# Token rows gathered as whole float32, a two-group place second, side products in single runs, and clock-keeping products ahead of the counts

## The chip, the cores and the metric

The kernel runs on one core of one Trainium2 chip. The core has TensorE (PE: matmuls, PEld: the loads of their stationary operand), VectorE (DVE), ScalarE (ACT), GpSimd (POOL) and SyncE (SP), which here issues the transfers of weights. The metric is the time of one execution on the device in microseconds (us), the median of three runs.

## The reference

Two consecutive decoder layers over x of 256 tokens × 1024 channels in float32. The first has a convolution module and a linear recurrence side by side and a dense SwiGLU; the second a short convolution and block-sparse attention side by side, and then the part that the change concerns, top-2-of-8 SwiGLU experts:

```python
def moe_swiglu(h, router_w, router_b, wg, wu, wd):
    logits = xf.astype(F32) @ router_w.astype(F32) + router_b.astype(F32)
    top_logit, top_e = lax.top_k(logits, TOP_K)
    top_w = jax.nn.softmax(top_logit, axis=-1)
    ...
    def expert_block(args):
        xb, e = args
        return (jax.nn.silu(xb @ wg[e]) * (xb @ wu[e])) @ wd[e]
    ...
    out = jnp.zeros((n_tok, d), F32).at[row_tok].add(ys.astype(F32) * row_w[:, None])
```

`wg` and `wu` of an expert are 1024 × 3584, `wd` is 3584 × 1024, all float32: 42 MiB an expert, 336 MiB for the eight. Each is read once in each execution.

## The kernel before

The weights come as a stream of units (class `Stream`). An expert has 46 units: 16 of 1 MiB for the first 512-wide pieces of gate and up (phase 0 is gate, phase 1 up, 8 units each), 16 of 768 KiB for the 384-wide pieces (phases 2 and 3), and 14 of 1 MiB for `wd`. They land in slots of a ring; there are RING = 10 slots, and MORE = 6 more (`grow`) from the second half on. `fill` issues on SP's queue, in order, the transfer of unit n + ring as soon as PE has finished unit n (`finish`); the transfer is line 338.

The experts are ranked by their token counts, and a *place* is a position in the order in which they are computed. A place has room for two or three groups of 32 rows (`NGS`): an expert with few tokens goes to a place of two groups. `RANKS` says which rank by count goes to which place. The expert of the first place is guessed from the router's bias well before the counts (`S.first`), so its transfers can start early; the others are known once the counts are made, and SP reads their positions from `offs` (`values_load`, line 1279) and waits for it there.

In a place, each unit of gate and up runs with matmuls of four column groups, 128 × 32 stationary (`up`, line 1424), 24 records a unit with three groups, 16 with two. A float32 matmul leaves two records in the trace, one of type float32r (kept to its first part) leaves one. `down_e` (lines 1438 and 1445) does the same for `wd`.

Around these units stand *side products*, attached to the units by `after(e, phase, unit, f)`, which runs `f` behind that unit's matmuls of place e:

- `gather_bank` (line 1340): the rows of x of the next place or pair of places are gathered by a product with a matrix of ones and zeros, `G` (line 1315). The rows are held as two float32r parts, `hrh` and `hrl`, so each of the four banks has four products with the one and four with the other. `first_gather` does it for the first place.
- `backs` (lines 1377 and 1379): the transposes of `G` and the token weights, with which results go back.
- `scatter` (line 1404): the result of a place is added to x while the next place runs.

Ahead of the first place stands the routing: the last router products (line 1175), the selection `sel` on DVE (lines 1241 to 1243), the counts and the position of each token in its expert's rows by small products with `sel` (lines 1247 to 1252), `pos` (line 1254), `G`, and the gather. `keep_warm(20, …)` (line 550) issues 20 products whose result nobody reads, behind these small products. The scheduler puts instructions into an engine's row by readiness and priority; parts of it are pinned to the written order.

## Time and profile before

| | us |
|---|---|
| median of three runs (1347.02 to 1351.15) | 1349.56 |
| time of the profiled execution | 1347.33 |
| its span | 1345.6 |
| PE busy | 1274.1 (95%) |
| DVE busy | 492.8 (37%) |
| ACT busy | 301.6 (22%) |

The transfers moved 472.20 MB at a mean of 349 GB/s over the span. A busy PE is not a PE at its peak. Of the chain that ended last, PE has 80% and transfers 12%. The places of the experts begin on PE at 489.93, 605.66, 717.30, 801.89, 913.72, 1031.71, 1122.97 and 1240.23 us, and the last place's products end at 1335.2. Rows of a timeline group neighbouring instructions of one kind, with xN records; their busy times overlap a little, since matmuls are pipelined.

### The profile page before, as it was taken

How to read it: one execution, taken by the hardware profiler on the slowest of the kernel's cores; microseconds unless marked ns; L12 is line 12 of the kernel's file. 1: busy time of each engine (PE TensorE's matmuls, PEld its weight loads, DVE VectorE, ACT ScalarE, POOL GpSimd, SP SyncE). 2: the span in 40 equal slices, each digit the busy share in tenths (PEclk: the TensorE clock that was granted, in tenths of full speed). 3: DMA queues.
4: the chain of work that ended last, by engine and by line, in shares of the span. 5: the costliest groups of instructions: out<-in, count | busy, mean ns of one | idle time of the engine just before them, and what ended most of it. 6: DMA issues, size and time to landing. Idle time of an engine off the chain costs nothing.

```text
span 1345.6 us, 29781 instructions
## 1 busy us (share of the span) xinstructions
PE 1274.1 (95%) x12884; PEld 759.1 (56%) x12884; DVE 492.8 (37%) x1064; ACT 301.6 (22%) x623; POOL 1.2 (0%) x23
## 2 busy tenths in 40 slices
PE   4999999999999999999999999999999979999976
PEld 3878899999988863463354423353445312345321
DVE  8699998888777330101102001102101101100100
ACT  3175555555755322000001100000100000100000
POOL 0000000000000000000000000000000000000000
PEclk6998899999999979999999999999999999999999
DMA  9955999888400957999999999999999999999996
GB/s 380 401 200 210 360 372 357 306 339 342 180 7 33 373 220 256 384 417 405 358 417 417 417 419 417 416 418 417 416 418 416 416 419 419 414 417 417 401 414 232
DMA packets 72282, 472.20 MB, mean 351 GB/s; under 512 B 8272, under 2 KB 10320, under 8 KB 27856
## 3 DMA queue, kind: packets, MB, share of 16 engines
q1 hardware_dynamic: 72144, 470.22, 86.8%
q8 instruction: 103, 1.69, 0.5%
q14 instruction: 35, 0.29, 0.1%
HBM read 469.14 MB, written 1.05 MB: 349 GB/s over the span
## 4 chain that ended last, share of the span: by engine, by line
PE 80%; DMA 12%; DVE 6%; ACT 2%; issue 0%; DVEq 0%; SPq 0%; ACTq 0%
PE acc L1424 17%; PE mm L1424 17%; DMA raw<-in_moe 12%; PE mm L1445 8%; PE acc L1445 5%; PE mm L483 4%; PE mm L485 4%; PE mm L484 4%; PE acc L484 3%; PE acc L485 3%; PE acc L483 3%; PE mm L504 2%; PE acc L521 2%; DVE raw L468 1%; PE mm L1340 1%; DVE cv L795 1%
## 5 line engine op out<-in xcount | busy, mean ns | idle before, releaser
L1424 PE MATMUL acc<-raw,xe 128*32 128x512 f32 (+1 forms) x2688 | 264.8, 541 | 3.4 <-DMA raw<-in_moe 3.4
L1424 PE MATMUL mm<-raw,xe 128*32 128x512 f32 (+1 forms) x2688 | 260.8, 540 | 6.3 <-DMA raw<-in_moe 6.3
L1424 PEld LDWEIGHTS mm<-raw,xe 128*32 128x32 f32 x2688 | 84.9, 110 | 168.8 <-issue 145.7
L1424 PEld LDWEIGHTS acc<-raw,xe 128*32 128x32 f32 x2688 | 82.9, 110 | 150.2 <-issue 133.5
L367 ACT CAST wh<-raw 128x512 fp32r<-128x512 f32 x200 | 121.7, 620 | 128.3 <-PE mm L484 76.4
L368 DVE TENSOR_TENSOR wl<-raw,wh 128x512 fp32r<-128x512 f32 x200 | 133.8, 689 | 43.6 <-ACT wh L367 35.5
L483 PE MATMUL mm<-hh,wh 128*128 128x256 f32 x496 | 140.5, 284 | 0.5 <-ACT xr L657 0.5
L484 PE MATMUL mm<-hlo,wh 128*128 128x256 f32 x496 | 140.1, 283 | 0.3 <-DVE hlo L620 0.3
L485 PE MATMUL mm<-hh,wl 128*128 128x256 f32 x496 | 140.0, 283 | 0.0
L468 DVE SCALAR_TENSOR_TENSOR raw<-raw,crow 128x1024 f32<-128x1024 f32 x96 | 114.4, 1221 | 0.0
L1445 PE MATMUL mm<-raw,wh 128*32 128x256 f32 x2016 | 109.3, 379 | 0.0
L483 PEld LDWEIGHTS mm<-hh,wh 128*128 128x128 f32 x496 | 94.5, 191 | 1.4 <-ACT xr L657 0.7
L485 PEld LDWEIGHTS mm<-hh,wl 128*128 128x128 f32 x496 | 94.4, 190 | 1.1 <-issue 1.1
L484 PEld LDWEIGHTS mm<-hlo,wh 128*128 128x128 f32 x496 | 94.4, 191 | 1.1 <-issue 0.6
L1556 DVE TENSOR_TENSOR wl<-wl,acc 128x512 f32<-128x512 f32 (+1 forms) x22 | 13.1, 597 | 219.4 <-PE acc L1424 219.4
L1445 PEld LDWEIGHTS mm<-raw,wh 128*32 128x32 f32 x2016 | 65.4, 110 | 44.0 <-issue 1.2
L1556 DVE TENSOR_TENSOR wl<-wl,mm 128x512 f32<-128x512 f32 (+1 forms) x20 | 12.0, 598 | 181.3 <-PE mm L1424 181.3
L1445 PE MATMUL acc<-raw,wh 128*32 128x256 f32 x1344 | 72.9, 379 | 0.0
L1438 PE MATMUL acc<-raw,wh 128*32 128x512 f32 x448 | 54.3, 598 | 16.3 <-DMA raw<-in_moe 15.2
L504 PE MATMUL mm<-hh,raw 128*128 128x256 f32 x256 | 59.1, 393 | 4.0 <-ACT hh L612 4.0
L1445 PEld LDWEIGHTS acc<-raw,wh 128*32 128x32 f32 x1344 | 43.7, 110 | 29.3 <-issue 0.8
L504 PEld LDWEIGHTS mm<-hh,raw 128*128 128x128 f32 x256 | 50.4, 198 | 12.1 <-ACT hh L612 4.9
(346 smaller groups left out, 1225.2 us busy)
## 6 DMA issues: line engine op xcount, KB each, us to landing
raw<-in_moe SPq DMA_DIRECT2D x236, 1024.0 KB, 19.8
raw<-in_wst SPq DMA_DIRECT2D x109, 1024.0 KB, 7.0
raw<-in_moe SPq DMA_DIRECT2D x128, 768.0 KB, 15.0
raw<-in_moe SPq DMA_DIRECT2D x8, 512.0 KB, 14.7
x<-in_xt SPq DMA_DIRECT2D x1, 1024.0 KB, 5.0
out<-x SPq DMA_DIRECT2D x8, 128.0 KB, 2.7
gw<-in_gates SPq DMA_DIRECT2D x1, 512.0 KB, 19.5
mask<-in_const SPq DMA_DIRECT2D x1, 192.0 KB, 5.1
```

The costliest lines, as they stand in the source:

```text
L367: self.nc.scalar.copy(h, t[:, j:j + PART])
L368: self.nc.vector.tensor_tensor(l, t[:, j:j + PART], h.bitcast(F32), op=OP.subtract)
L468: nc.vector.scalar_tensor_tensor(src, src, 1.0, crow, op0=OP.mult, op1=OP.mult, accum_out=raw_mod[pre][:, 2 * n + b:2 * n + b + 1])
L483: nc.tensor.matmul(o, wh, xh, start=first, stop=False, skip_group_check=skip)
L484: nc.tensor.matmul(o, wh, xl, start=False, stop=False, skip_group_check=skip)
L485: nc.tensor.matmul(o, wl, xh, start=False, stop=last, skip_group_check=skip)
L504: nc.tensor.matmul(o, wh, xh[:, k], start=(cb == 0 and k == 0), stop=(k == KB - 1), skip_group_check=True)
L521: nc.tensor.matmul(o, wh, yf[:, k], start=st, stop=sp, skip_group_check=True)
L1424: nc.tensor.matmul(ps[j * GROUP:(j + 1) * GROUP, :width], xe[:, k, r * GROUP:(r + 1) * GROUP], w[:, j * width:(j + 1) * width], start=(k = ...
L1438: nc.tensor.matmul(yb[0][t * GROUP:(t + 1) * GROUP], hs[r], w[:, f * D + h * 512:f * D + (h + 1) * 512], start=first, stop=last, skip_grou ...
L1445: nc.tensor.matmul(yb[c // 2][t * GROUP:(t + 1) * GROUP, c % 2 * 256:c % 2 * 256 + 256], hs[r], w[:, f * D + q * 256:f * D + q * 256 + 256 ...
L1556: nc.vector.tensor_tensor(h, h, ps[:, :width], op=OP.mult)
```

## The change

The rows to be gathered are held once, as float32 (`hr`), so a bank has four float32 products instead of eight of float32r, and the six DVE operations that made `hrl` are gone. `keep_warm` stands ahead of the first products with `sel`, the count product behind `pos`. The places have two groups at 1, 4 and 7 (counted from 0) instead of 2, 5 and 7. Four gather banks stand behind one unit, so do the two `backs`, and the four scatter banks. The ring has MORE = 7, 17 slots in all.

```diff
...
-RING, AHEAD, PARTS, MORE, SPARE = 10, 3, 7, 6, 2
+RING, AHEAD, PARTS, MORE, SPARE = 10, 3, 7, 7, 2
...
-NGS = (3, 3, 2, 3, 3, 2, 3, 2)
-RANKS = (0, 1, 5, 2, 3, 6, 4, 7)
+NGS = (3, 2, 3, 3, 2, 3, 3, 2)
+RANKS = (0, 5, 1, 2, 6, 3, 4, 7)
...
-                        sq = ob.tile([P, 3, P], F32, name="sq", bufs=2)
+                        sq = ob.tile([P, 3, P], F32, name="sq")
...
-    hrh = mo.tile([P, 2, D], F32R, name="hrh")
-    hrl = mo.tile([P, 2, D], F32R, name="hrl")
+    hr = mo.tile([P, 2, D], F32, name="hr")
...
-        rests = []
         for g in range(3):
             for t in range(2):
                 r, n = row(t, g)
-                hh, hlo = (a[:, t, g * 384:g * 384 + n * P].rearrange("p (b c) -> p b c", b=n)
-                           for a in (hrh, hrl))
-                nc.scalar.activation(hh, r[:, :, :P], AF.Copy, scale=rr[:, t:t + 1])
-                rests.append((hlo, r[:, :, :P], rr[:, t:t + 1], hh.bitcast(F32)))
+                o = hr[:, t, g * 384:g * 384 + n * P].rearrange("p (b c) -> p b c", b=n)
+                nc.scalar.activation(o, r[:, :, :P], AF.Copy, scale=rr[:, t:t + 1])
...
-        chosen = nc.vector.tensor_scalar(sel, sel, 1.5, None, op0=OP.is_lt)
-
+        nc.vector.tensor_scalar(sel, sel, 1.5, None, op0=OP.is_lt)
+
+        keep_warm(WARM[1], ident, x[:, KB - 1, :P])
         pp = acc_bank()
-        for t in range(2):
-            nc.tensor.matmul(pp[:, 2 * NE:3 * NE], one_pp, sel[:, t], start=(t == 0), stop=(t == 1))
-
         below = con("below")
         nc.tensor.matmul(pp[:, :NE], below, sel[:, 0], start=True, stop=True)
         nc.tensor.matmul(pp[:, NE:2 * NE], below, sel[:, 1], start=True, stop=False)
@@ -1254,10 +1248,12 @@
         nc.vector.scalar_tensor_tensor(pos, pp[:, :2 * NE].rearrange("p (t e) -> p t e", t=2), 1.0,
                                        sel, op0=OP.add, op1=OP.mult)
 
+        for t in range(2):
+            nc.tensor.matmul(pp[:, 2 * NE:3 * NE], one_pp, sel[:, t], start=(t == 0), stop=(t == 1))
+
         t0 = mo.tile([P, 2, NE], F32, name="hid0")
         nc.vector.tensor_tensor(t0, pos, lead_[:, None].to_broadcast([P, 2, NE]), op=OP.mult)
         nc.vector.tensor_reduce(posp[:, :, 0], t0, axis=AX.X, op=OP.add)
-        keep_warm(WARM[1], ident, x[:, KB - 1, :P])
         nc.vector.tensor_copy(cnt, pp[:, 2 * NE:3 * NE])
...
-        tile_ = mo.tile([P, 2, 2 * P], F32R, name="G")
+        tile_ = mo.tile([P, 2, 2 * P], F32, name="G")
...
-    def gather_parts(ps, G, g, parts):
+    def gather_products(ps, G, g):
         n = G.shape[2]
-        for part in parts:
-            for j in range(2):
-                b = 2 * g + j
-                for t in range(2):
-                    nc.tensor.matmul(ps[:, j * n:(j + 1) * n], part[:, t, b * P:(b + 1) * P],
-                                     G[:, t], start=(part is hrh and t == 0 and j == 0),
-                                     stop=(part is hrl and t == 1), skip_group_check=True)
+        for j in range(2):
+            b = 2 * g + j
+            for t in range(2):
+                nc.tensor.matmul(ps[:, j * n:(j + 1) * n], hr[:, t, b * P:(b + 1) * P], G[:, t],
+                                 start=(t == 0 and j == 0), stop=(t == 1), skip_group_check=True)
...
-        gather_parts(ps, G, g, (hrh, hrl))
+        gather_products(ps, G, g)
...
-        pss = [acc_bank() for _ in range(4)]
         for g in range(4):
-            gather_parts(pss[g], G, g, (hrh,))
-        for g in range(4):
-            gather_parts(pss[g], G, g, (hrl,))
+            ps = acc_bank()
+            gather_products(ps, G, g)
             for j in range(2):
-                scaled(xe[:, 2 * g + j], pss[g][:, j * n:(j + 1) * n], 2 * g + j, g % 2 == 0)
+                scaled(xe[:, 2 * g + j], ps[:, j * n:(j + 1) * n], 2 * g + j, g % 2 == 0)
...
-        for i, (o, r, sc, h) in enumerate(rests):
-            with tc.issue_after(chosen.ins if i < 2 else placed[-1].ins):
-                nc.vector.scalar_tensor_tensor(o, r, sc, h, op0=OP.mult, op1=OP.subtract)
...
         after(e, 1, 0, begin)
-        for g in range(4):
-            after(e, 1, 1 + g, lambda g=g: gather_bank(
-                [(lambda b, n=n: xes[n][:, b], CAPS[n]) for n in es], st["G"], g, side_bank()))
-        for i, n in enumerate(es):
-            after(e, 1, 5 + i, lambda n=n: backs(n, st["of"]))
+
+        def rows():
+            for g in range(4):
+                gather_bank([(lambda b, n=n: xes[n][:, b], CAPS[n]) for n in es], st["G"], g,
+                            side_bank())
+
+        def both():
+            for n in es:
+                backs(n, st["of"])
+
+        after(e, 1, 1, rows)
+        after(e, 1, 5, both)
...
         if e < NE - 1:
             rows_ = expert_rows(yb, bks[e][1])
-            for g in range(4):
-                after(e + 1, 0, 2 + g,
-                      lambda g=g, a=rows_, b=bks[e][0], n=NGS[e]: scatter(g, *a, b, n))
+
+            def back_to_x(a=rows_, b=bks[e][0], n=NGS[e]):
+                for g in range(4):
+                    scatter(g, *a, b, n)
+
+            after(e + 1, 0, 3, back_to_x)
...
...
```

`keep_warm` itself is as it was: products of `ident` with a piece of x, 128 × 128 by 128 columns.

The row of PE at the routing, before; L1175 are the last router products, L1247 to L1252 those with `sel`, L550 the clock-keeping ones, L1340 the gather of the first place, L1424 the first expert's. One row can stand for two records of the trace.

```order
L1175 MATMUL acc<-turn_w,x 128x136 x4
L1247 MATMUL acc<-sel,one_pp 128x8 x2
L1250 MATMUL acc<-sel,below 128x8
L1251 MATMUL acc<-sel,below 128x8
L1252 MATMUL acc<-sel,one_pp 128x8
L550 MATMUL acc<-x,sm_o 128x128 x5
L1340 MATMUL acc<-G,hrh 128x96 x4
L1340 MATMUL acc<-G,hrl 128x96 x4
L1340 MATMUL acc<-G,hrh 128x96 x12
```

...and after, where L1244 to L1246 and L1252 are the products with `sel`, L1333 the gather and L1413 the first expert's:

```order
L1175 MATMUL acc<-turn_w,x 128x136 x4
L550 MATMUL acc<-x,sm_o 128x128 x20
L1244 MATMUL acc<-sel,below 128x8
L1245 MATMUL acc<-sel,below 128x8
L1246 MATMUL acc<-sel,one_pp 128x8
L1252 MATMUL acc<-sel,one_pp 128x8 x2
L1333 MATMUL acc<-G,hr 128x96 x16
L1413 MATMUL mm<-raw,xe 32x512 x24
```

The 20 clock-keeping products have moved ahead of all products with `sel`, the count product (L1252) behind the three for `pos`, and nothing stands between the gather and the first expert.

The row of PE in phase 1 of the first place, before: units (L1424) and gather banks (L1340) in turn.

```order
L1424 MATMUL acc<-raw,xe 32x512 x24
L1340 MATMUL mm<-G,hrh 128x160 x4
L1340 MATMUL mm<-G,hrl 128x160 x4
L1424 MATMUL acc<-raw,xe 32x512 x12
L1340 MATMUL mm<-G,hrh 128x160 x4
L1340 MATMUL mm<-G,hrl 128x160 x4
L1424 MATMUL acc<-raw,xe 32x512 x12
L1340 MATMUL mm<-G,hrh 128x160 x4
L1340 MATMUL mm<-G,hrl 128x160 x4
L1424 MATMUL acc<-raw,xe 32x512 x12
```

After, the units (L1413), the gather in one run (L1333) and the `backs` (L1366, L1368):

```order
L1413 MATMUL acc<-raw,xe 32x512 x24
L1333 MATMUL mm<-G,hr 128x160 x16
L1413 MATMUL acc<-raw,xe 32x512 x48
L1366 MATMUL mm<-sm_o,G 128x128 x2
L1368 MATMUL mm<-wtsp,G 128x1 x2
L1366 MATMUL mm<-sm_o,G 96x128 x2
L1368 MATMUL mm<-wtsp,G 96x1 x2
```

The four banks and the two `backs` have moved together, each behind one unit.

The row of SP at its wait for `offs`, before; each transfer is one unit, and 128x2048 is a unit of 1 MiB. The first row shown is the 9th transfer of the first expert, the wait is that of the row "ISA" with three semaphores. Rows between the transfers are its address arithmetic.

```order
L338 DMA raw<-in_moe 128x2048 [waits DMAHW1_49]
L338 DMA raw<-in_moe 128x2048 [waits DMAHW2_49]
L338 DMA raw<-in_moe 128x2048 [waits DMAHW3_49]
L338 DMA raw<-in_moe 128x2048 [waits DMAHW4_49]
L338 ISA [waits DVE_49,Pool_49,Activation_49]
L338 DMA raw<-in_moe 128x2048 [waits DMAHW5_49,DVE_49]
L338 DMA raw<-in_moe 128x2048 [waits DMAHW6_49,DVE_49]
L338 DMA raw<-in_moe 128x2048 [waits DMAHW7_49,PE_49]
```

After, from the same place:

```order
L338 DMA raw<-in_moe 128x2048 [waits DMAHW1_49]
L338 DMA raw<-in_moe 128x2048 [waits DMAHW2_49]
L338 DMA raw<-in_moe 128x2048 [waits DMAHW3_49]
L338 ISA [waits Activation_49,DVE_49]
L338 DMA raw<-in_moe 128x2048 [waits DMAHW4_49]
L338 DMA raw<-in_moe 128x2048 [waits DMAHW5_49]
L338 DMA raw<-in_moe 128x2048 [waits DMAHW6_49,DVE_49]
L338 DMA raw<-in_moe 128x2048 [waits DMAHW7_49,DVE_49]
L338 DMA raw<-in_moe 128x2048 [waits DMAHW0_49,PE_49]
```

The wait has moved ahead of one transfer, and the first transfer with a wait on PE stands behind four others instead of two.

## Rows read from the trace of the kernel before

**Rows 1.** The page, the span in 40 equal slices of 33.6 us: the granted clock of TensorE in tenths, and what the transfers moved.

```profile
PEclk6998899999999979999999999999999999999999
GB/s 380 401 200 210 360 372 357 306 339 342 180 7 33 373 220 256 384 417 405 358 417 417 417 419 417 416 418 417 416 418 416 416 419 419 414 417 417 401 414 232
```

**Rows 2.** The windows by stage (us from the span's start): length, busy us and count of PE, PEld, DVE, ACT and POOL, then the granted clock, the share of the transfer engines and GB/s.

```profile
471.00:482.50 11.50, 8.68 (x41) 8.71 (x42) 8.13 (x35) 5.01 (x11) 0.00 (x0) 0.50 0.08 17
482.50:492.50 10.00, 10.00 (x67) 8.11 (x70) 3.06 (x14) 0.75 (x2) 0.00 (x0) 0.72 0.96 403
492.50:515.00 22.50, 22.50 (x214) 7.12 (x210) 0.69 (x2) 3.50 (x6) 0.00 (x0) 1.00 0.80 280
515.00:547.50 32.50, 32.50 (x320) 13.38 (x316) 3.97 (x6) 6.24 (x20) 0.00 (x0) 1.00 0.70 250
547.50:630.00 82.50, 82.50 (x1160) 38.76 (x1156) 9.49 (x20) 4.57 (x9) 0.00 (x0) 1.00 1.01 417
630.00:660.00 30.00, 30.00 (x316) 10.12 (x312) 3.97 (x6) 0.14 (x1) 0.00 (x0) 1.00 0.93 336
660.00:802.00 142.00, 139.71 (x1736) 59.95 (x1732) 14.86 (x30) 12.23 (x31) 0.00 (x0) 1.00 1.01 418
802.00:1032.00 230.00, 230.00 (x2964) 102.01 (x2967) 26.06 (x51) 14.22 (x35) 0.00 (x0) 1.00 1.01 417
```

**Rows 3.** The waits of SP's queue between 431 and 530: the waiting line, whom it waited for, us in total, times, the longest.

```profile
SPq L1279 <- DVE offs L1277: 27.5, 1, 27.5
SPq L338 <- PE mm L1424: 24.6, 8, 9.7
```

**Rows 4.** The chain that ended last, from 570 on: start, length, what it was, and how many records.

```profile
605.66 7.72 PE acc L1424 x72
629.48 20.60 PE mm L1424 x192
650.08 15.48 PE acc L1424 x192
681.04 36.26 PE acc L1445 x672
717.30 5.15 PE mm L1424 x48
...
763.39 18.42 DMA raw<-in_moe
781.94 19.82 DMA raw<-in_moe
801.89 7.93 PE acc L1424 x72
```

**Rows 5.** The timeline of PE in the routing: start, busy us, engine, line, operation, records, and the idle time before it with its releaser.

```profile
468.32 1.21 PE L1175 MATMUL acc<-turn_w,x 128*128 128x136 f32 x8 [0.58 <-DVE x L680]
473.82 0.99 PE L1247 MATMUL acc<-sel,one_pp 128*128 128x8 f32 x4 [4.28 <-ACT hrh L1231]
...
475.94 2.48 PE L550 MATMUL acc<-x,sm_o 128*128 128x128 f32 x10
478.07 1.07 PE L1340 MATMUL acc<-G,hrh 128*128 128x96 f32 x4
...
482.36 1.05 PE L1340 MATMUL acc<-G,hrl 128*128 128x96 f32 x4
...
488.65 1.34 PE L550 MATMUL acc<-x,sm_o 128*128 128x128 f32 x10
489.93 5.36 PE L1424 MATMUL mm<-raw,xe 128*32 128x512 f32 x48
```

**Rows 6.** Short windows around the routing, columns as in group 2.

```profile
470.00:471.00 1.00, 0.00 (x0) 0.00 (x0) 0.63 (x5) 0.69 (x4) 0.00 (x0) 1.00 0.72 295
471.00:472.00 1.00, 0.00 (x0) 0.00 (x0) 0.83 (x6) 0.25 (x2) 0.00 (x0) 0.50 0.10 41
476.00:480.00 4.00, 4.00 (x20) 4.00 (x20) 3.74 (x16) 0.00 (x0) 0.00 (x0) 0.50 0.00 0
488.00:489.00 1.00, 1.00 (x11) 1.00 (x10) 0.14 (x1) 0.00 (x0) 0.00 (x0) 0.97 1.06 451
```

**Rows 7.** The timeline of DVE in the routing.

```profile
473.50 0.17 DVE L1243 TENSOR_SCALAR sel<-sel 128x16 f32<-128x16 f32 x1
...
476.13 0.17 DVE L1254 SCALAR_TENSOR_TENSOR pos<-acc,sel 128x16 f32<-128x16 f32 x1 [1.41 <-PE acc L1252]
...
476.75 0.36 DVE L1315 TENSOR_TENSOR G<-iota,posp 128x192 fp32r<-128x192 f32 x1
477.02 1.14 DVE L1485 SCALAR_TENSOR_TENSOR hrl<-mm,rs,hrh 128x384 fp32r<-128x384 f32 x2
...
480.14 0.16 DVE L1277 TENSOR_SCALAR offs<-of 1x8 int32<-1x8 f32 x1
```

**Rows 8.** The timeline of PE where side products stand between the units of the first expert, and below it a row of the chain, of a projection near the start: start, length, what, records.

```profile
517.62 2.78 PE L1424 MATMUL acc<-raw,xe 128*32 128x512 f32 x24
520.33 0.68 PE L1340 MATMUL mm<-G,hrh 128*128 128x160 f32 x4
...
521.38 2.78 PE L1424 MATMUL acc<-raw,xe 128*32 128x512 f32 x24
...
35.68 22.73 PE mm L504 x104
```

More of the change, by code (lines that the diff above doesn't have):

```diff
@@ L1296, in weights @@
         by_place(wtsp, wts, 2)
-    placed = []
     def place(es):
-        tile_ = mo.tile([P, 2, 2 * P], F32R, name="G")
+        tile_ = mo.tile([P, 2, 2 * P], F32, name="G")
         at, of = 0, {}
@@ L1314, in place @@
             of[e] = tile_[:, :, at:at + n * cap]
-            placed.append(nc.vector.tensor_tensor(
+            nc.vector.tensor_tensor(
                 of[e].rearrange("p t (i s) -> p t i s", i=n),
                 iota[:, None, None, :cap].to_broadcast([P, 2, n, cap]),
-                posp[:, :, None, e:e + 1].to_broadcast([P, 2, n, cap]), op=OP.is_equal))
+                posp[:, :, None, e:e + 1].to_broadcast([P, 2, n, cap]), op=OP.is_equal)
         return once, of
@@ L1363, in first_gather @@
         n = G.shape[2]
-        pss = [acc_bank() for _ in range(4)]
         for g in range(4):
-            gather_parts(pss[g], G, g, (hrh,))
-        for g in range(4):
-            gather_parts(pss[g], G, g, (hrl,))
+            ps = acc_bank()
+            gather_products(ps, G, g)
             for j in range(2):
-                scaled(xe[:, 2 * g + j], pss[g][:, j * n:(j + 1) * n], 2 * g + j, g % 2 == 0)
+                scaled(xe[:, 2 * g + j], ps[:, j * n:(j + 1) * n], 2 * g + j, g % 2 == 0)
     def back(e, G, ps):
-        G = G.bitcast(F32)
         cap = G.shape[2]
@@ L1619, in rest @@
             units = expert_units(0)
-            G = mo.tile([P, 2, 2 * P], F32R, name="G")[:, :, :P]
+            G = mo.tile([P, 2, 2 * P], F32, name="G")[:, :, :P]
             nc.vector.tensor_tensor(G, iota[:, None, :].to_broadcast([P, 2, P]),
@@ L1626, in rest @@
                             acc_bank())
-            Gf = G.bitcast(F32)
             ps = acc_bank()
             for t in range(2):
-                nc.tensor.transpose(ps[:, t * P:(t + 1) * P], Gf[:, t], ident)
+                nc.tensor.transpose(ps[:, t * P:(t + 1) * P], G[:, t], ident)
             for t in range(2):
-                nc.tensor.matmul(ps[:, T:T + 1], Gf[:, t], wts[:, t, 0:1], start=(t == 0),
+                nc.tensor.matmul(ps[:, T:T + 1], G[:, t], wts[:, t, 0:1], start=(t == 0),
                                  stop=(t == 1))
```

## The prediction

> **What bounds the kernel now.** I first read the page's slices: from the 18th on the core moves 417 GB/s or nearly so, with a dip to 358 in the 20th, and the 15th, in which the experts begin, has a granted clock of 0.7 [rows 1]. Then come the windows by stage, the waits of SP, and the chain. The expert weights are 8 × 46 units = 336 MiB. In the undisturbed windows the core moves 417 to 418 GB/s [rows 2], so a unit of 1 MiB costs 2.51 us and an expert of 42 MiB 105.5 us. TensorE needs for an expert of three groups 2 × 20.6 + 2 × 15.5 + 36.3 = 108.5 us [rows 4] plus its side products; two groups run two thirds of the matmuls, about 72.3 us. So a three-group place lets the transfers run ahead until the ring is full, and a two-group place eats that lead and then waits for DMA: in place 2 the chain goes over to transfers at 763.39 and stays there until 801.89 [rows 4]. The end is therefore set by the transfers, and what they lose counts, wherever it is. A stretch loses its length × (1 − its GB/s / 417.5). By [rows 2] that is 11.0 us in 471 to 482.5, 7.4 in 492.5 to 515, 13.0 in 515 to 547.5 and 5.8 in 630 to 660; the windows of 802 to 1032 lose nothing.
>
> The reasons are two. First the routing: TensorE's last product before it starts at 468.32 and the next at 473.82 [rows 5]; the granted clock falls from 1.00 to 0.50 at 471 and is back only at 488 [rows 6], so the small products, the keep-warm ones and the gather of the first expert all run at half rate, and the first expert begins at 489.93 [rows 5]. SP waits 27.5 us for the expert offsets and then 24.6 us in eight waits for a unit that TensorE has finished [rows 3]. From then to 547.5 the ring is full and one transfer starts for each unit computed. There the transfers are paced by TensorE, and in the phases whose units are 768 KiB a unit takes 15.48 / 8 = 1.94 us, while it releases a slot for a unit of 1 MiB or a smaller one. Second, place 1 is again one of three groups, finds the ring nearly full, and the same pacing shows at 630 to 660, at 336 GB/s [rows 2].
>
> **The change, part by part.**
>
> *Start of the first expert.* The 20 keep-warm products (40 records) move from behind the counts to behind the last router product, which ends near 469.5. At full rate a record of 128 columns takes 0.107 us; I get this from the last ten, 1.34 us with pipelining [rows 5]. 40 of them end at about 473.8, where `sel` is ready (473.50 + 0.17) [rows 7], so they delay nothing. Before `pos` there are now six records instead of ten. At half rate the ten took from 473.82 to 475.94, 0.21 each [rows 5]; at full rate six take 0.6, and with 0.2 us to DVE `pos` stands at about 474.65 instead of 476.13 [rows 7]. The count product goes behind it (four records; DVE reads the count once `pos` is made). From `pos` to the end of `G` there were 476.13 to 477.11 [rows 7], plus the wait for the later counts: `G` is there at about 476.2. The gather is 16 float32 products, two records each, 32 records as before (32 products with one record each). At half rate twenty records took from 478.07 to 482.36, 0.21 each [rows 5]; at full rate 32 × 0.107 = 3.4. So the first expert product comes at 479.7, 10.2 us earlier. Bounds: if the clock dips in the wait for `G` and half of the gather runs at 0.21, 1.7 us later, a gain of 8.5. I take the middle, 9.35. The 6 operations on DVE that made `hrl` are gone; four of them stood between `G` and the offsets, two of 1.14 us together among them [rows 7], so the offsets come at about 477.8 instead of 480.14 + 0.16.
>
> *SP.* It issues 11 transfers before it waits for the offsets, before it was 12, and 6 behind the wait that need no unit of the first expert, before it was 4. The pause of the transfers thus begins a unit (2.5 us) earlier and ends 2.4 us earlier: it moves and keeps its length. The gain of the start isn't lost by it: TensorE needs the twelfth unit only 11 × 2.58 = 28 us after it starts, near 508, long after its landing. What follows the pause is paced by TensorE until 547.5, so there the start's gain passes on to the transfers us for us.
>
> *One more slot.* 17 slots instead of 16: each transfer goes out one unit earlier while TensorE paces them. At the end of that stretch, a unit is 1.94 us [rows 4], at its start 2.58. Gain 1.9, at most 2.6; below, nothing if the ring was no limit, which the eight waits [rows 3] exclude. The room for it comes from the second half of `hrh`/`hrl` and one `sq` buffer; that buffer costs at most a wait in the scans of the router, ahead of 468, on ACT and DVE that TensorE's own products cover.
>
> *Order of the places.* Two groups second: its 72 us of TensorE against 105.5 us of transfers empties the ring, so that nothing is full at 630 to 660. That gives back 5.8 us, or 4.5 if I start the ring at its level at the end of the first place; I take 5.15. Places 2 and 3 are then a pair of three groups behind a two-group place, as the pair of 801.89 to 1032 was, and that pair ran at 417 [rows 2]. Nothing is charged for them.
>
> *Side products.* Gather of a three-and-two pair: four banks in one run of 32 float32 records of 160 columns. Before, a bank stood between two units of the expert: 521.38 − 517.62 = 3.76 for a unit of 2.58 and 8 records, so 1.18 a bank [rows 8]. The nearest float32 row with wide tiles is L504, 22.73 us / 104 = 0.219 for 256 columns [rows 8]; by columns this is 0.137 for 160. So 32 × 0.137 = 4.4 us, against 4 × 1.18 = 4.7. What a single run saves is thus the time between two tilings, 1.18 − 8 × 0.137 = 0.09 a time: 0.3 with the gather, 0.1 with the two `backs`. It counts only in the first place, where TensorE paces: 0.4. Elsewhere the transfers hide it, and if that cover were gone it would be under 1 us a place. Bounds: 0 and 1. A long run stops the release of slots for 4.7 us; the ring has 17 units (43 us) in hand, hence no charge.
>
> *Sum.* 9.35 + 1.9 + 5.15 + 0.4 = 16.8. Against the profiled execution's own 1347.33 this is 1330.5. The median of the runs shown, 1349.56, is 2.2 above that one; I add half: 1331.6, said as **1332**. The bounds of the terms (8.5 + 1.9 + 4.5 + 0 to 10.2 + 2.6 + 5.8 + 1) give 14.9 to 19.6, hence 1327.7 to 1332.4, up to 1334.6 by the median: own range 1327 to 1336.
>
> **A rule against the row.** That early keep-warm products hold the clock is not shown by the trace. What it shows speaks rather against it: PE was busy 1.00 of 476 to 480, and the clock stood at 0.50 until 488 [rows 6]; so 14 us of small products from 473.82 did not keep or lift it at once. The Trainium skill, page "TensorE: Matmul & The Clock Gate", section "Part 1: The HAM clock gate", says that the throttled clock is the default and that activity releases it; an engine that is never let idle would by it stay at 2.4 GHz. The row's fall came at 471, after 1.5 us of idle, with which this agrees; the row's late return is what makes me doubt. By the one the start gains 10.2 us, by the other 2.7 (second rival).
>
> **The rivals.**
>
> 1. *The forecast*, 1332: chance 0.60.
>
> 2. *The clock falls all the same* (the change doesn't do what it says): the keep-warm products don't count as enough, the clock falls at 471, and what is left of them runs at 0.21: 14 are done by 471, 26 take 5.5 us, to 476.6, and now the counts wait for them. Then `pos` at 478.2, `G` at 480.5, gather 32 × 0.21 = 6.8: start 487.2. The start gains 2.7, the sum 2.7 + 1.9 + 5.15 + 0.4 = 10.15: 1337.2, by the median 1339.4. For it: the long stay at 0.50 [rows 6]. Against: the clock was 1.00 while small products ran with idle gaps, up to 471. Chance 0.20.
>
> 3. *The pairs of three groups refill the ring* at places 3 and 6, and the pause of 630 to 660 only moves: 5.15 comes back once or twice, 1337 to 1343. For it: TensorE needs more per three-group place (717.30 − 605.66 = 111.6 in place 1 [rows 4]) than the transfers (105.5). Against: the pair at 802 to 1032 ran at 417 [rows 2]. Chance 0.07.
>
> 4. *The transfers don't hold 417* when no pause lets them catch up: at 411, between the 418 and the 403 of [rows 2], 336 MiB take 13 us more, and 3.8 of the gain stay: 1343.5, by the median 1345.8, no change that can be told. Only the waits for DMA at 763 to 802, two chain pieces of 18 to 20 us [rows 4], make me think of it. Chance 0.05.
>
> 5. *Slower*: as in 2, but the clock stays at 0.50 into the first expert. A unit then takes 5.15 instead of 2.58 us, in a stretch that paces the transfers, so half of each us at half rate is lost. It eats the 10.15 of rival 2 in 20.3 us, by about 507.5; beyond that the kernel is slower, with the clock back at 530 by 11 us (1358). For it: the clock needed 14 us to return, at 488 [rows 6]. Against: what brought it back were products like those that come here earlier. Chance 0.04.
>
> Left for what I don't see, still faster: 0.04. A measurement can tell 0.3% (4 us) from no change. Faster: 0.60 + 0.20 + 0.07 + 0.04 = 0.91; same 0.05; slower 0.04. The range goes from the lower end of the forecast, 1326.5, over rival 2 into the middle of rival 3, 1340.5, and leaves out some 0.15.
>
> **What the profile after would show.** PEclk 1.00 through 471 to 480, and the first expert product near 480 (rival 2: near 487). 11 transfers before SP's wait for the offsets, which ends near 478. DMA at 417 in the 30 us around 640 and PE waiting for transfers inside place 1 and place 4. One run of 32 records, about 4.6 us, where four banks stood. I am wrong if the pause at full ring shows up in another place, if the f32 records take much more than 0.14 us, or if PEclk is 0.5 anywhere behind 490.

## The result, and the profile after

The changed kernel takes **1333.22 us** (median of 4 runs, 1332.04 to 1334.43) against 1349.32 of the kernel before in the same comparison: ratio 0.9882, 95% interval 0.9864 to 0.9899, so 16 us or 1.2% faster. The profiled execution has 1332.04 us with a span of 1330.3. Two slow executions of kernels below, of 3298 and 2216 us at a mean clock of 0.39 and 0.60, are left out of all medians and ratios.

The page after, the two rows that answer to [rows 1]:

```profile
PEclk7899899999999999999999999999999999999999
GB/s 381 398 211 182 355 373 374 308 340 328 187 56 1 329 272 317 400 417 414 419 419 417 417 417 417 417 417 417 416 420 418 414 417 419 404 417 417 407 417 234
```

In the 15th slice the granted clock is 0.9 or more where it was 0.7, and from the 18th on no slice but the 35th and 38th, and the tail, is below 413 GB/s; the dip of the 20th is gone.

The windows, columns as in [rows 2]: first four short ones in the routing, then those that answer to [rows 2].

```profile
477.00:478.00 1.00, 0.36 (x3) 0.39 (x4) 0.93 (x7) 0.00 (x0) 0.00 (x0) 1.00 0.00 0
478.00:479.00 1.00, 1.00 (x10) 1.00 (x10) 0.86 (x6) 0.22 (x1) 0.00 (x0) 0.87 0.06 16
479.00:482.00 3.00, 3.00 (x16) 3.00 (x16) 1.35 (x7) 0.53 (x2) 0.00 (x0) 0.50 0.62 161
482.00:483.00 1.00, 1.00 (x13) 0.91 (x12) 0.00 (x0) 0.90 (x3) 0.00 (x0) 0.93 1.00 418
482.50:492.50 10.00, 10.00 (x95) 3.64 (x98) 3.17 (x14) 3.54 (x7) 0.00 (x0) 1.00 1.02 428
492.50:515.00 22.50, 22.50 (x203) 9.61 (x196) 0.00 (x0) 5.78 (x17) 0.00 (x0) 1.00 1.00 397
515.00:547.50 32.50, 32.50 (x360) 12.22 (x356) 3.97 (x6) 3.39 (x11) 0.00 (x0) 1.00 0.81 301
630.00:660.00 30.00, 29.44 (x334) 10.46 (x328) 2.26 (x5) 0.98 (x2) 0.00 (x0) 1.00 1.02 418
660.00:802.00 142.00, 137.36 (x1684) 59.37 (x1680) 14.54 (x29) 11.30 (x30) 0.00 (x0) 1.00 1.01 417
802.00:1032.00 230.00, 220.55 (x2488) 87.47 (x2484) 25.76 (x53) 15.51 (x37) 0.00 (x0) 1.00 1.01 417
```

The stretch behind the routing moves 397 and 301 GB/s where it moved 280 and 250, and 630 to 660 is at 418 instead of 336. The clock falls late: 0.87 in 478 to 479, 0.50 until 482 and 0.93 after it, which puts the fall at about 478.7 and the return at 482.1. TensorE is busy throughout that time; in the second before (477 to 478) it was busy for 0.36.

SP's waits from 431 to 530 after (columns as in [rows 3]; `mm` and `acc` are the two kinds of buffer that TensorE's products write), and below them the wait of before that belongs to those of [rows 3]:

```profile
SPq L1275 <- DVE offs L1273: 26.9, 1, 26.9
SPq L338 <- PE acc L1413: 18.2, 6, 6.7
SPq L338 <- PE mm L1413: 17.9, 8, 3.0
```

```profile
SPq L338 <- PE acc L1424: 13.7, 5, 3.2
```

The wait for the offsets is 26.9 us and the waits for finished units 36.1 (before, 24.6 + 13.7 = 38.3): SP still waits for TensorE, which paces the transfers there.

TensorE in the routing after, to be read beside [rows 5]:

```profile
469.47 1.21 PE L1175 MATMUL acc<-turn_w,x 128*128 128x136 f32 x8 [0.58 <-DVE x L680]
470.52 4.63 PE L550 MATMUL acc<-x,sm_o 128*128 128x128 f32 x40
...
476.21 0.61 PE L1252 MATMUL acc<-sel,one_pp 128*128 128x8 f32 x4 [0.27 <-DVE pos L1248]
477.64 5.41 PE L1333 MATMUL acc<-G,hr 128*128 128x96 f32 x32 [0.82 <-DVE key L1264]
482.98 5.36 PE L1413 MATMUL mm<-raw,xe 128*32 128x512 f32 x48
```

The 40 clock-keeping records end at 475.13, where `sel` is ready, the gather follows the counts without anything between, and takes 5.41 us. The last router product starts at 469.47 instead of 468.32 [rows 5]: code ahead of the routing is the same but for one buffer, and part of the delay is already there early on: the row of L504 in [rows 8] took 22.73 us before, at a granted clock of 1.00, and 25.78 in this execution, in which the clock stood at 0.50 from 35 to 41.8. The buffer is not the cause, since two further executions of the changed code reach this product at 468.32 and 468.33. Executions differ by this, 468.3 to 470.8 in the profiles below. So from here on starts are counted from that product: before, the first expert starts 489.93 − 468.32 = 21.61 us behind it, after 13.51, a gain of 8.10. To the end of the span it is 1345.6 − 468.32 = 877.3 and 860.8: 16.45 us.

The chain after, start and length, pieces that answer to [rows 4]:

```profile
509.68 4.54 PE mm L1333 x32
...
610.97 14.22 DMA raw<-in_moe
...
659.80 19.82 DMA raw<-in_moe
...
961.51 19.24 DMA raw<-in_moe
```

The gather of 160 columns is one piece of 4.54 us. From 610.97 the chain goes over transfers: place 1, of two groups, waits for them where place 2 did before.

### The profile page after: what moved, and what is told of

Read it like the earlier page. It is cut to its first block, busy times and chain, and to the rows that moved or that the text cites. A ratio compares the mean times of both kernels' runs of the same rounds, so it can differ in the third digit from the quotient of the medians.

```text
span 1330.3 us, 29774 instructions
## 1 busy us (share of the span) xinstructions
PE 1261.5 (95%) x12884; PEld 757.4 (57%) x12884; DVE 487.9 (37%) x1058; ACT 300.8 (23%) x623; POOL 1.2 (0%) x23
## 4 chain that ended last, share of the span: by engine, by line
PE 73%; DMA 19%; DVE 6%; ACT 1%; issue 0%; DVEq 0%; SPq 0%; ACTq 0%
DMA raw<-in_moe 19%; PE mm L1413 15%; PE acc L1413 15%; PE acc L1434 5%; PE mm L1434 5%; PE mm L483 4%; PE mm L485 4%; PE mm L484 4%; PE acc L484 3%; PE acc L485 3%; PE acc L483 3%; PE mm L504 2%; PE acc L521 2%; DVE raw L468 1%; PE mm L1333 1%; DVE cv L795 1%
## 5 line engine op out<-in xcount | busy, mean ns | idle before, releaser
L1413 PE MATMUL acc<-raw,xe 128*32 128x512 f32 (+1 forms) x2688 | 259.7, 540 | 3.0 <-DMA raw<-in_moe 3.0
L1413 PE MATMUL mm<-raw,xe 128*32 128x512 f32 (+1 forms) x2688 | 257.8, 540 | 3.8 <-DMA raw<-in_moe 3.8
L1413 PEld LDWEIGHTS mm<-raw,xe 128*32 128x32 f32 x2688 | 86.6, 110 | 168.6 <-issue 154.2
L1413 PEld LDWEIGHTS acc<-raw,xe 128*32 128x32 f32 x2688 | 85.3, 110 | 164.5 <-issue 147.8
L504 PE MATMUL mm<-hh,raw 128*128 128x256 f32 x256 | 61.0, 402 | 5.1 <-ACT hh L612 3.3
L504 PEld LDWEIGHTS mm<-hh,raw 128*128 128x128 f32 x256 | 51.7, 203 | 13.9 <-ACT hh L612 6.1
## 6 DMA issues: line engine op xcount, KB each, us to landing
gw<-in_gates SPq DMA_DIRECT2D x1, 512.0 KB, 19.7
```

What stands on the lines that cost most here:

```text
L504: nc.tensor.matmul(o, wh, xh[:, k], start=(cb == 0 and k == 0), stop=(k == KB - 1), skip_group_check=True)
L1413: nc.tensor.matmul(ps[j * GROUP:(j + 1) * GROUP, :width], xe[:, k, r * GROUP:(r + 1) * GROUP], w[:, j * width:(j + 1) * width], start=(k = ...
```

## The experiments

The table has for each kernel the median, the ratio to the kernel before with its interval, and from the profile the start of the first expert and the end of the span, both counted from the start of the last router product ("start", "to end"). The kernels were timed in three groups, on three chips, and each ratio is to the kernel before in its own group (1348.8, 1349.3 and 1349.0 us). "By the ratio" below means a difference of two ratios times 1349 us. A row without the word "before" is the changed kernel with what the row names.

| kernel | median us | ratio (95%) | start | to end |
|---|---|---|---|---|
| before | 1349.3 | 1 | 21.61 | 877.3 |
| changed | 1333.2 | 0.9882 (0.9864 to 0.9899) | 13.51 | 860.8 |
| changed, again | 1333.1 | 0.9882 (0.9867 to 0.9896) | 13.50 | 860.8 |
| no clock-keeping products | 1334.5 | 0.9891 (0.9874 to 0.9908) | 14.86 | 862.7 |
| these in the old place | 1338.7 | 0.9927 (0.9914 to 0.9939) | 19.23 | 867.1 |
| these, and 4 more in the waits | 1331.3 | 0.9871 (0.9857 to 0.9886) | 11.68 | 859.4 |
| old order of places | 1336.3 | 0.9905 (0.9889 to 0.9922) | 13.50 | 865.3 |
| 16 slots | 1335.3 | 0.9891 (0.9873 to 0.9909) | 13.50 | 864.1 |
| side products in parts | 1334.3 | 0.9884 (0.9866 to 0.9903) | 13.50 | 862.1 |
| gather a phase later | 1329.5 | 0.9849 (0.9833 to 0.9865) | 13.50 | 858.0 |
| offsets' wait later | 1334.2 | 0.9887 (0.9872 to 0.9902) | 13.50 | 860.6 |
| filled, and side products later | 1329.0 | 0.9844 (0.9830 to 0.9857) | 11.68 | 856.5 |
| before, no clock-keeping products | 1345.1 | 0.9962 (0.9949 to 0.9976) | 15.90 | 874.9 |
| before, new order of places | 1345.7 | 0.9971 (0.9960 to 0.9981) | 21.64 | 872.3 |

The changed kernel repeats within 0.1 us in the last two columns, which makes them finer than the medians. But each is read from a single profiled execution, and "to end" holds whatever that execution lost later on: in the run "before, no clock-keeping products" it is off by 1.6 us from this. So a difference of under 2 us in it rests on one execution.

Where the kernels differ can be read from the transfers as well. In the 85 us behind the last router product the kernel before moves 260 GB/s, the changed one 314 (317 when repeated) and, with 16 slots, 302. By the prediction's own rule, length × (1 − GB/s / 417.5), that is 32.1 us lost before, 20.5 to 21.1 after, 23.5 with 16 slots. From 125 to 205 us behind that product it is 5.8 us before, 0.3 after, and 5.3 with the old order of places.

> The changed kernel as it is, once more, so that the kernels of this call can be set against it on one chip. Expected: the same 16 us under the kernel before (1333), the first expert product 13.5 us behind the start of the last router product (469.47 to 482.98 before), the granted clock down to 0.50 for about 3.5 us in the gather.

### What moved the start: the clock, or the row of TensorE

The first edit takes the 20 products of the routing out, the second puts them back into their old place in the code.

```diff
-        keep_warm(WARM[1], ident, x[:, KB - 1, :P])
         pp = acc_bank()
...
         nc.vector.tensor_reduce(posp[:, :, 0], t0, axis=AX.X, op=OP.add)
+        keep_warm(WARM[1], ident, x[:, KB - 1, :P])
```

(The first has only the line with the minus, the second both.)

> The changed kernel without the 20 clock-keeping products of the routing. Theory A (what moved the start is that 40 records left the way between the counts and the first expert; the clock is a smaller part): the clock falls about 1.5 us after the last router product, the counts and the whole gather run at 0.21 us a record, gather about 6.9 instead of 5.4 us, counts 1 us later: first expert product about 2 us later than in the changed kernel, time +2 (1335). Theory B (the clock held by the early products is the gain): the start falls back by most of the 7 us won, +6 or more (1339).

> The changed kernel with the 20 clock-keeping products back in their old place in the code, behind the counts; in the row of TensorE 3 of them then stand ahead of the gather and 17 between the gather and the first expert. Theory A: 40 records at 0.21 us or, once the clock is back, 0.11 us stand in the way again: first expert product 7 to 9 us later than in the changed kernel, and the time as much longer (1340 to 1342). Theory B: the clock falls as in the run without these products, so about the same as that run.

TensorE in the run without them:

```profile
476.32 0.57 PE L1243 MATMUL acc<-sel,below 128*128 128x8 f32 x2 [4.44 <-ACT hr L1228]
...
478.01 1.02 PE L1251 MATMUL acc<-sel,one_pp 128*128 128x8 f32 x4 [0.27 <-DVE pos L1247]
479.64 5.96 PE L1332 MATMUL acc<-G,hr 128*128 128x96 f32 x32 [0.61 <-DVE key L1261]
485.53 5.36 PE L1412 MATMUL mm<-raw,xe 128*32 128x512 f32 x48
```

And in the run with them in the old place:

```profile
478.88 6.28 PE L1333 MATMUL acc<-G,hr 128*128 128x96 f32 x32
484.99 3.99 PE L550 MATMUL acc<-x,sm_o 128*128 128x128 f32 x34
488.91 5.36 PE L1413 MATMUL mm<-raw,xe 128*32 128x512 f32 x48
```

The clock in the run without them, in two windows:

```profile
474.00:484.00 10.00, 6.80 (x31) 6.67 (x31) 5.83 (x29) 4.98 (x10) 0.00 (x0) 0.50 0.14 38
484.00:486.00 2.00, 2.00 (x20) 1.61 (x23) 0.40 (x3) 0.75 (x2) 0.00 (x0) 0.95 1.03 426
```

Without the products the clock is at 0.50 from 474 to 484, but the start loses only 1.36 us (14.86 against 13.50). In the old place 34 of the 40 records stand between the gather and the first expert, 3.99 us, and 6 ahead of the gather; the start is 5.7 us later than in the changed kernel and the time 5.6 us more (6.1 by the ratio). In both runs the clock is at 0.50 from 474 to 484, so their difference, 19.23 − 14.86 = 4.4 us, is what it is worth that nothing stands in the way any more, and 1.4 us is what the early products add to that by the clock: theory A. The gain of the start, 8.10, is thus 4.4 + 1.4, and the 21.61 − 19.23 = 2.4 that are left belong to the rest of the change (the gather as float32, the count product behind `pos`, the operations on DVE that are gone). No run puts these back one by one, and in the run with the old place the clock also came back earlier than before (14.6 us behind the last router product instead of 19.7), so how the 2.4 divide stays open. The 1.36 us are less than the 2 expected because in that run, too, the clock is back at 484 before the gather ends.

The same from the other side, the kernel before with only these products left out:

```diff
-        keep_warm(WARM[1], ident, x[:, KB - 1, :P])
```

> The kernel before with one thing left out, the 20 clock-keeping products behind the counts. By what the runs without and with these products showed: the 40 records no longer stand between the counts and the first expert, the gather runs at 0.21 us a record from 477.2 and the first expert starts near 484 instead of 489.93: -5 to -6 against the kernel before (1343.5). Rival: without them the clock comes back later, the first expert starts at half rate, and the gain is less than 3.

```profile
481.81 3.18 PE L1339 MATMUL acc<-G,hrl 128*128 128x96 f32 x14
484.92 7.13 PE L1423 MATMUL mm<-raw,xe 128*32 128x512 f32 x48
```

```profile
486.00:488.00 2.00, 2.00 (x13) 0.39 (x8) 1.47 (x8) 0.00 (x0) 0.00 (x0) 0.50 1.05 438
488.00:490.00 2.00, 2.00 (x20) 0.56 (x16) 0.00 (x0) 0.00 (x0) 0.00 (x0) 0.86 0.98 406
```

The start comes 5.7 us earlier, but the first two units then take 7.13 us instead of 5.36 [rows 5], since the clock is back only at about 488, as before. That leaves 3.9, which is what the medians give (1349.0 − 1345.1); by the ratio it is 5.1 (3.2 to 6.9). From the last router product to the end only 2.4 us are won: in the 85 us behind that product the transfers lose 28.0 instead of 32.1 us (280 GB/s instead of 260), which is a gain of 4.1, but in this execution they lose 1.6 us more than before at the very end, from 760 us behind that product on (352 GB/s instead of 359). Both theories had a part: the row was in the way, and once it is free the slow clock costs 1.8 us in the first expert.

### The waits in which the clock falls

```diff
             nc.tensor.matmul(pp[:, 2 * NE:3 * NE], one_pp, sel[:, t], start=(t == 0), stop=(t == 1))
+        keep_warm(4, ident, x[:, KB - 1, :P])
```

> The changed kernel with 4 more clock-keeping products, put by the scheduler in two pairs into the two waits of TensorE (for the positions, 0.27 us, and for the gather matrix, 0.82 us). If those waits are what lets the clock fall in the gather: the clock stays 1.00, the gather takes 3.4 to 3.6 instead of 5.4 us, the first expert starts 1.5 to 2 us earlier, time -2 (1331). If the kind of work counts (8-column products) and not the wait, the clock falls all the same and nothing is won (within 0.5 us).

TensorE and, below, the windows from 478 on:

```profile
477.24 0.69 PE L550 MATMUL acc<-x,sm_o 128*128 128x128 f32 x4
478.00 3.78 PE L1334 MATMUL acc<-G,hr 128*128 128x96 f32 x32
481.71 5.36 PE L1414 MATMUL mm<-raw,xe 128*32 128x512 f32 x48
```

```profile
478.00:482.00 4.00, 4.00 (x36) 3.77 (x40) 2.88 (x14) 1.81 (x5) 0.00 (x0) 1.00 0.27 49
482.00:484.00 2.00, 2.00 (x24) 0.64 (x20) 1.14 (x6) 1.20 (x2) 0.00 (x0) 1.00 1.02 430
```

The clock stays 1.00, the gather takes 3.78 us instead of 5.41, and the start gains 1.8 us. In all seven profiled executions with the changed kernel's routing as it is, the clock falls 0.9 to 1.7 us into the gather; in both with the two waits of 0.27 and 0.82 us filled, this one and the last kernel below, it does not. So filling these waits is what holds it. Whether the idle time in them lets it fall, or that there was little work in that stretch (8-column products alone), no run separates: the added products change both. Against a clock that is down from 474 on, a clock that holds is worth 14.86 − 11.68 = 3.2 us in the start. The 3.4 us of the prediction were near for a clock that holds.

### The order of the places

```diff
-NGS = (3, 2, 3, 3, 2, 3, 3, 2)
-RANKS = (0, 5, 1, 2, 6, 3, 4, 7)
+NGS = (3, 3, 2, 3, 3, 2, 3, 2)
+RANKS = (0, 1, 5, 2, 3, 6, 4, 7)
```

> The changed kernel with the order of places of the kernel before (two groups at places 2, 5 and 7). My step: the second place, again of three groups, finds the ring nearly full, the transfers fall to about 340 GB/s for 30 us somewhere in 620 to 660, and 4.5 to 5.8 us come back: 1338 (+5). Rival: the pause was owed to the later start of the first expert and is gone with it, then no change (1333).

> The kernel before with the new order of places alone. The pause at 630 to 660 (5.8 us lost) is gone, as in the changed kernel: -4 to -5 (1344.5). Rival: with the later start and one slot less, another place fills the ring and the loss moves there: under -2.

The window of 620 to 650, with the old order in the changed kernel:

```profile
620.00:650.00 30.00, 30.00 (x316) 10.03 (x311) 3.97 (x6) 0.60 (x1) 0.00 (x0) 1.00 0.96 344
```

and that of 630 to 660 in the kernel before with the new order:

```profile
630.00:660.00 30.00, 30.00 (x348) 11.16 (x344) 4.83 (x8) 0.98 (x2) 0.00 (x0) 1.00 1.02 416
```

The old order brings the pause back, at 344 GB/s, and costs 4.5 us to the end (3.1 by the ratio); the new order alone takes it out of the kernel before, 416 instead of 336 [rows 2], and gains 4.9 us to the end (3.9 by the ratio, 2.6 to 5.4). The order is worth 3 to 5 us in both kernels, whatever the start. The transfers say the same: 5.3 us lost with the old order against 0.3.

### The seventeenth slot, and the side products

Each run puts one part of the change back: MORE = 6, and the `after` calls as before.

> The changed kernel with 16 slots instead of 17. My step: one unit of 1.94 us while TensorE paces the transfers, so +1.9 (1335), at most +2.6. Rival: the slot only fills the pause of the routing and is worth nothing (within 0.5 us).

> The changed kernel with the side products (gather banks, returns, scatter banks) behind several units again, as in the kernel before. My step: +0.4, only in the first place. Rival: tilings changed more often cost TensorE more in each place, and that counts in the three places that are not yet bound by transfers, +1 or more.

With 16 slots 3.3 us are lost to the end, 2.2 by the medians and 1.2 by the ratios; with the side products in parts 1.25, 1.2 and 0.3. Both go the way of my steps, and in the profiles further: the slot was priced 1.9, the parts 0.4. The chain of the run with the side products in parts, in phase 1 of the first place:

```profile
511.03 1.28 PE mm L1333 x8
512.32 2.71 PE acc L1413 x24
515.03 1.28 PE mm L1333 x8
```

The four banks are 1.28 us each, 5.12 against one run of 4.54, and each unit behind a bank takes 2.71 instead of 2.61 (four units in a row were 10.44). That makes 1.00 us for three more interruptions, so one (into the other tiling and back) costs 0.33 and not 0.09. With the two `backs` the whole phase takes 1.2 us longer, which is all of the 1.25. For the slot, the transfers above lose 2.4 to 3.0 us more with 16. The times alone can tell neither from no change.

### Which lost transfers count

The offsets are read by SP behind the 17th transfer of the first expert:

```diff
-                self.nc.sync.dma_start(t[:, s], src[:, s])
+                self.sent.append(self.nc.sync.dma_start(t[:, s], src[:, s]))
...
+    def offsets():
+
+        with tc.issue_after(S.sent[S.dense + S.ring - 1].ins):
+            S.offs = [nc.values_load(offs[:1, i:i + 1], engines=(mybir.EngineType.SP,), min_val=0,
...
+    after(0, 1, 7, offsets)
```

> The changed kernel with SP's wait for the expert offsets behind the 17th transfer of the first expert instead of the 11th (the offsets are needed only from the 47th on). Six transfers then go out at about 470 instead of 480, and the pause of the transfers in the routing, which loses 9.8 us at 470 to 480, is mostly filled. Theory (the ring is full soon after, so TensorE's units and the number of slots set where the transfers stand at 550): no change, within 1 us (1333), the loss only moves to 482 to 510. Rival (each us in which nothing is transferred counts): -8 to -9 (1324.5).

The windows of this run, and below them the same of the changed kernel, then a line of SP's waits from 431 to 530 in this run:

```profile
470.00:482.50 12.50, 11.41 (x85) 11.12 (x85) 6.72 (x35) 5.31 (x16) 0.00 (x0) 0.86 1.01 419
482.50:510.00 27.50, 27.50 (x254) 8.96 (x253) 3.17 (x14) 5.35 (x10) 0.00 (x0) 1.00 0.77 274
510.00:547.50 37.50, 37.50 (x395) 16.47 (x397) 3.97 (x6) 7.38 (x23) 0.00 (x0) 1.00 0.76 293
```

```profile
470.00:482.50 12.50, 11.41 (x85) 11.11 (x85) 6.73 (x35) 5.32 (x16) 0.00 (x0) 0.86 0.20 60
482.50:510.00 27.50, 27.50 (x254) 8.97 (x254) 3.17 (x14) 5.33 (x10) 0.00 (x0) 1.00 1.01 410
510.00:547.50 37.50, 37.50 (x396) 16.50 (x398) 3.97 (x6) 7.38 (x23) 0.00 (x0) 1.00 0.83 313
```

```profile
SPq L339 <- PE mm L1418: 31.4, 8, 16.6
```

The pause of the routing is gone, 419 instead of 60 GB/s, and the time is the same: 860.6 us to the end against 860.8. What was moved earlier is missing later, 274 instead of 410 GB/s at 482.5 to 510, and SP waits 31.4 us instead of 17.9 for those units. While the ring is full, only TensorE's units and the number of slots say where the transfers stand at 550; the pause ahead of that stretch is free.

So in the first place TensorE's time counts, and that of its side products too. The next edit moves the gather run and the two returns of place 0 into its phase 2, in which TensorE finishes units faster than they can be fetched:

```diff
-        after(e, 1, 1, rows)
-        after(e, 1, 5, both)
+        after(e, 1 + (e == 0), 1, rows)
+        after(e, 1 + (e == 0), 5, both)
```

> The changed kernel with the gather run and the two returns of the first place behind units of its phase 2 instead of phase 1; the other places are as they were. If the end is set by what the transfers lose while TensorE paces them, then the 4.54 and 0.7 us of these products cost transfers in phase 1 (they release units of 1 MiB and 768 KiB at 2.58 us) but not in phase 2, where 1.94 us a unit releases units of 1 MiB that take 2.51: -4 to -5 (1328.5). If they are hidden in phase 1 as well, no change; if the later rows make the second place wait, slower.

```profile
510.00:547.50 37.50, 37.50 (x396) 16.73 (x392) 3.97 (x6) 7.38 (x23) 0.00 (x0) 1.00 0.94 351
530.00:540.00 10.00, 10.00 (x114) 5.19 (x112) 0.00 (x0) 4.23 (x14) 0.00 (x0) 1.00 0.82 298
```

351 GB/s instead of 313 in 510 to 547.5, which is (351 − 313) / 417.5 × 37.5 = 3.4 us of transfers; 2.9 us to the end are won, 4.4 by the ratio. That is less than the 4.54 + 0.7 moved. The run now stands behind the second unit of phase 2, and the transfers still fall to 298 GB/s at 530 to 540, so this stretch still waits for TensorE. A place some units later may give the rest; that wasn't tried.

The last kernel has both edits, and the return of place 0's own matrix in phase 2 as well:

```diff
+        keep_warm(4, ident, x[:, KB - 1, :P])
...
-        after(e, 1, 0, begin)
+        after(e, 1 + (e == 0), 0, begin)
...
-    after(0, 0, 1, lambda: backs(0, G0))
+    after(0, 2, 0, lambda: backs(0, G0))
```

> The changed kernel with the 4 more clock-keeping products of the run before, and with all side products of the first place (the return of its own matrix, the gather run, the two returns) in its phase 2. By the two runs apart: -1.6 for the clock, -3 to -4 for the gather, -0.7 for the return of phase 0: -5.5 to -6.5 (1327). If the transfers are already at their rate in that stretch, less: the clock's part is lost, -4 (1329).

```profile
470.00:482.50 12.50, 12.43 (x109) 11.22 (x112) 7.54 (x38) 6.91 (x17) 0.00 (x0) 1.00 0.17 57
510.00:547.50 37.50, 37.50 (x398) 17.05 (x394) 4.67 (x8) 7.82 (x25) 0.00 (x0) 1.00 0.95 378
```

The clock stays 1.00 in the routing, and the second window moves 378 GB/s instead of 313. 4.3 us are won to the end, which is the 1.45 and the 2.86 of the two edits, and nothing for the return; the expected 5.5 was too much by this count (the ratio gives 5.1). At 1329.0 us, ratio 0.9844 (0.9830 to 0.9857), it is the fastest kernel here, 20 us under the kernel before and 4 under the changed one; from the run with the gather alone moved (1329.5) it can't be told by the medians.

## Why the prediction was right

The time, 1333.2, lies in the forecast's own range (1327 to 1336), and the first case came true, with parts of the second in the gather. By its steps:

- *Start of the first expert*, 9.35: measured 8.10, below the lower bound of 8.5. The keep-warm products end at `sel`, as said, and the clock stays 1.00 until 478.7, past the 471 of rival 2. Then it dipped, as the lower bound allowed, and by as much: the gather took 5.41 us against 3.78 with the clock held, 1.6 more where the bound had 1.7. The forecast took half of that dip, and it came whole: this is 0.85 of the 1.25 that are missing. The rest is the price of a record. The 0.107 does not follow from the row that it was read from (1.34 us for ten, or 489.93 − 488.65 = 1.28 to the next row); measured are 4.63 us for the 40 records, 0.116 each, and the same in the gather with the clock held. That is 0.3 us over the gather, which also began 0.3 later behind the router than reckoned (8.17 us instead of 7.9); against these stand 0.2 of a shorter dip and of rounding. With the waits filled the start gains 21.61 − 11.68 = 9.9, near the 10.2 of the upper bound. The reason behind the number was not the one that I had weighed most: of the 8.10 the runs give 4.4 to the freed row, 1.4 to the early products by the clock, and 2.4 to the rest of the change. In the prediction the freed row was only implied, as the 40 records that are gone from between the gather and the first expert. Rival 2 did not come. That the start passes on to the end us for us came true nearly: 1.36 us of it cost 1.9 to the end, 5.7 cost 6.3, and a gain of 1.8 gave 1.45.
- *The rule and the row*: the clock held from 470.5, through the early products and the short waits behind them, and fell at 478.7; with the waits filled it held throughout. The doubt that I drew from [rows 6], that small products don't hold the clock, was wrong for a clock that is up: those of [rows 6] had started at a clock that was already down, and there it took until 488 to come back. The page "TensorE: Matmul & The Clock Gate" of the Trainium skill says in its section "Part 1: The HAM clock gate" that the throttled clock is the default and that activity releases it. The traces agree in that the clock came back with TensorE at work, at 484 and at 488, and held through the 40 early records; that it fell at 478.7 with TensorE busy again after two short waits, and took 14 us to come back before, goes beyond that sentence.
- *SP*: right. 11 transfers ahead of the wait, offsets 478.89 − 469.47 = 9.4 us behind the router instead of 11.8 [rows 5, 7], a gain of 2.4; the pause kept its length. But the sentence that what the transfers lose counts, wherever it is, was wrong: the run with the later wait takes the pause away and wins nothing. The error did not reach the sum, because the pause was priced at nothing for another reason, that it moves and keeps its length.
- *One more slot*, 1.9, at most 2.6: measured 3.3 to the end, 2.4 to 3.0 by the transfers of the same execution, 1.2 by the ratios; how much of it holds over several executions stays open.
- *Order of the places*, 5.15: measured 4.5 and 4.9 to the end (3.1 and 3.9 by the ratios), nearest to the lower bound, which starts the ring at its level at the end of the first place; the transfers of the first of these runs give 5.0. The pause is gone, no other place fills the ring (rival 3), and the pair of 2 and 3 ran at 417. The transfers held 417 to 418 in the long windows (rival 4).
- *Side products*, 0.4, bounds 0 and 1: measured 1.25 to the end and 1.2 in the chain of the first place, 0.3 by the ratios. The run of 32 records took 4.54 us, 0.142 each, as said (4.4 to 4.7); an interruption was priced at 0.09 and is 0.33.
- *The signs of the profile after*: the clock was to be 1.00 through 471 to 480, and it fell at 478.7; the first expert came at 482.98 and not near 480. The others came true: 11 transfers ahead of the wait, 418 GB/s at 630 to 660, transfers in the chain inside places 1 and 4 (from 610.97 and 961.51), and no fall of the clock from 490 to the last 5 us.

The four measured parts, 8.1 + 4.5 + 3.3 + 1.25 = 17.1, stand against 16.45 for the whole. The start was priced 1.25 us too high and the order 0.7, the slot and the side products 2.2 too low; that the sum of 16.8 is so near is in part luck, because these cancel. By the ratios the last three come to 4.6 instead of 9.0, and some 3 us of the 16 would belong to no part; so the whole is sure, and its division among these three is known to 1 or 2 us only.

## What to carry to other kernels

Work that keeps an engine awake is paid for where it stands in that engine's row: put it into waits, never between a result and its reader; here four products in gaps of under 1 us added 1.8 us to the start's gain, more than the 1.4 of the twenty ahead of them (the four alone weren't tried). Lost transfer time counts only where nothing later makes the transfers wait anyway (the pause of 10 us here was free), so before filling a pause look whether the ring is full behind it. Where one engine paces a full ring, a product that moves to a stretch paced by the transfers can be time won: here 2.9 us for the 5.2 that were moved first, and nothing for the return of 0.7 moved after them.

## What was not expected of the hardware

The granted clock fell to 0.50 with TensorE busy: at about 478.7, 1.1 us after the gather had begun (0.9 to 1.7 in the seven executions with that routing), following two waits of 0.27 and 0.82 us, and was back 3.4 us later. After the longer idle time it stayed down much longer, with TensorE at work from 473.82 to 488 [rows 5, 6] and, without the early products, from 476.3 to 484. Two executions of the same code ahead of the routing differ by up to 2.5 us at its last product; a part of this is the clock near the start, at 0.50 in the first 6 us of one projection in one execution and 1.00 throughout it in another.
